# Retention in a two-layer token mixer: 272 keys in tiles of 128, 128 and 16 instead of 128, 72 and 72

## The chip, the cores and the metric

The kernel runs on one core of a Trainium2 chip. The metric is the device time of one execution in microseconds (us), lower is better. TensorE does the matrix products, and what the profile calls PEld is its loading of weights, which overlaps the products. VectorE (DVE), ScalarE (ACT) and GpSimd (POOL) do the elementwise work, and SyncE (SP) issues most transfers. Each engine runs its own list of instructions strictly in order, and waits on semaphores of the others.

## The reference

Two layers run over 272 tokens (16 learned ones, then 256 real ones) of width 2048. Of each layer the change touches the retention, with 8 heads of 128 key columns and 256 value columns:

```python
q = rotary(q, pos) * (RET_DK ** -0.5)
k = rotary(k, pos)
scores = jnp.einsum('bhid,bhjd->bhij', qi, ki) * decay      # causal, decays with i - j
inner  = jnp.einsum('bhij,bhjv->bhiv', scores, vi)
y_ret  = head_group_norm(retention, gn_g) * silu(g_ret)
...
merged = sigmoid(m_ret) * (y_ret @ w_branch[0]) + sigmoid(m_conv) * (y_conv @ w_branch[1])
h      = h + merged @ w_out
```

The reference goes through chunks with a carried state; the kernel computes the same thing over all pairs (i, j) with j <= i at once. All projections (q, k, v, the gates and the convolution's inputs) come from one 2048 x 18432 matrix per layer. Everything is float32.

## The kernel before, in words

The tokens stand along the free dimension. The work is a list of **blocks**, one for each 128 output columns of a weight matrix. A block loads its 128 x 2048 weights in two halves (`raw`), splits each into a rounded high part `wh` (a ScalarE copy, L127) and a rest `wl` (a VectorE subtraction, L128), and runs 48 or 32 matmuls over 16 slices of the input (L153, L156, L170). TensorE works through the blocks one after the other. The weights of a block are loaded and split two blocks ahead.

For each head of a layer there are six blocks (k, q, two of v, two of gates). After the first gate's block come the `scores`, after the second the `outputs` (in head 0 of layer 0 both are put two blocks later, `LATE`). Within `scores`:

- L291 makes the scores of the first 128 keys with three products of split operands (`products3`, L250). The other keys go through plain float32 products (L295): weights are the keys of a tile (72 columns), and the moving operand is the queries from the tile's first key on (144, then 72 columns). Each appears in the trace as two matmuls, each with its own weight load.
- L299 and L300 multiply by the decay and write `sc`. L300 does tiles 2 and 3 with one instruction: 72 partitions, 144 + 72 = 216 columns.
- L307 transposes the values with TensorE, two transposes for each tile; the weights are the tile's tokens (128 or 72 columns), and 128 columns of an identity move.
- L311 (ScalarE) and L312 (VectorE) take the mean out of each tile's values, and `halves` splits the first tile's (`hi<-v` on ScalarE, `lo<-v` on VectorE).

In `outputs`, for each half of the value columns, three split products of the first tile (L250: weights `hi`, `hi`, then `lo` of the values) and two plain float32 products for tiles 2 and 3 (L327: weights are 72 x 128 values, 144 and 72 columns of `sc` move) add up in one PSUM bank.

The table `JT` holds, for each tile, the first key, the number of keys and the column where its scores begin in `sc`; `SC` is the number of columns of `sc` and of the decay table `dec`, 128 x `SC` for each head.

The order in which an engine runs its instructions is not that of the source: the framework lays it out when it builds the program, by its own estimate of when each instruction can start. A change of a shape can so move other instructions.

Of the kernel before, what the change touches and what calls it, by code (L numbers as in the profile page):

```python
# [18 lines left out]
L = SEQ + META  # L19
# [6 lines left out]
EPS = 1e-6  # L26
HALF = KC // 2

JT = ((0, 128, 0), (128, 72, 272), (200, 72, 416))
SC = 488  # L30


FIRST = 4
# [16 lines left out]
def hybrid_trunk(ctx: ExitStack, tc: tile.TileContext, xT, w_first, w_in, w_br, w_out, w_last, g_last, params, consts, dec, out):  # L50
# [13 lines left out]
    def new(name, cols=L):  # L64
        return tmp.tile([P, cols], F32, tag="t", name=name, padded_shape=[P, L])
# [78 lines left out]
    def product(parts, mov, c0, spare=False, narrow=False, midway=None):  # L144
        n = L - c0
        ps = psr.tile([P, 512], F32, name="pr") if spare else psm.tile([P, 512], F32, name="ps")
        if 2 * n <= 512 and not narrow:

            both = ps.rearrange("p (m n e) -> p m n e", m=2, e=2)
            for k in range(KC):  # L150
                wh, wl = parts[k // HALF]
                o = (k % HALF) * P
                nc.tensor.matmul(  # L153
                    both, wh[:, o:o + P], mov[:, k, :, :, c0 // 2:].rearrange("p e m n -> p m n e"), start=(k == 0), stop=False, skip_group_check=True
                )
                nc.tensor.matmul(  # L156
                    turns(ps[:, :n]), wl[:, o:o + P], part(mov, k, 0, c0),
                    start=False, stop=(k == KC - 1), skip_group_check=True,
                )
            b, a = new("pb", n), new("pa", n)  # L160
            nc.scalar.copy(b, ps[:, n:])  # L161
            nc.vector.tensor_tensor(out=a, in0=ps[:, :n], in1=b, op=ALU.add)  # L162
            return a
        for k in range(KC):
            if k == HALF and midway:
                midway()
            wh, wl = parts[k // HALF]
            o = (k % HALF) * P
            for i, (w, m) in enumerate(((wh, 0), (wh, 1), (wl, 0))):
                nc.tensor.matmul(  # L170
                    turns(ps[:, :n]), w[:, o:o + P], part(mov, k, m, c0),
                    start=(k == 0 and i == 0), stop=(k == KC - 1 and i == 2),
                )
        return ps[:, :n]
# [7 lines left out]
    def tt(out, a, b, op=ALU.mult):  # L182
        nc.vector.tensor_tensor(out=out, in0=a, in1=b, op=op)  # L183
# [53 lines left out]
    def halves(a, cols, moving=False):  # L237

        hi, lo = newr("hi", cols), newr("lo", cols)
        if moving:  # L240
            a, hi, lo = apart(a), hi.rearrange("p (e n) -> p e n", e=2), lo.rearrange("p (e n) -> p e n", e=2)
        nc.scalar.copy(hi, a)
        tt(lo, a, f32(hi), ALU.subtract)
        if moving:
            hi, lo = hi.rearrange("p e n -> p n e"), lo.rearrange("p e n -> p n e")
        return hi, lo

    def products3(out, w, m, stop=True):
        for i, (a, b) in enumerate(((0, 0), (0, 1), (1, 0))):
            nc.tensor.matmul(turns(out), w[a], m[b], start=(i == 0), stop=(stop and i == 2))  # L250

    def retention(layer, hd, i0, u, y):
# [33 lines left out]
        def scores():  # L286
            dt = decp.tile([P, SC], F32, name="dec")
            nc.sync.dma_start(dt, dec[hd])
            ps = psr.tile([P, 512], F32, name="pr")
            sc = scp.tile([P, SC], F32, name="sc")  # L290
            products3(ps[:, i0:L], st["kr"], st["qr"])  # L291
            for j0, nj, o in JT[1:]:
                lo = max(j0, i0)
                o += lo - j0
                nc.tensor.matmul(  # L295
                    ps[:nj, o:o + L - lo], st["k"][:, j0:j0 + nj], st["q"][:, lo - i0:L - i0],
                    start=True, stop=True,
                )
            tt(sc[:, i0:L], ps[:, i0:L], dt[:, i0:L])  # L299
            tt(sc[:72, L:SC], ps[:72, L:SC], dt[:72, L:SC])  # L300
            st["sc"] = sc
            st["scr"] = halves(sc[:, i0:L], L - i0, moving=True)
            pv = [psr.tile([P, 512], F32, name="pr") for _ in range(2)]
            vt = [pv[0][:, :DV], pv[0][:, DV:], pv[1][:, :DV]]
            for n, (j0, nj, _) in enumerate(JT):
                for c in range(2):
                    nc.tensor.transpose(vt[n][:nj, c * P:(c + 1) * P], st["v", c][:, j0:j0 + nj], ident)  # L307
            vv = []
            for n, (j0, nj, _) in enumerate(JT):
                v, sm = new("v", DV), new("vsum", 1)  # L310
                nc.scalar.activation(v[:nj], vt[n][:nj], AF.Copy, accum_out=sm[:nj])  # L311
                nc.vector.tensor_scalar(  # L312
                    out=v[:nj], in0=v[:nj], scalar1=float(DV), scalar2=sm[:nj], op0=ALU.mult, op1=ALU.subtract
                )
                vv.append(v)
            st["vr"] = halves(vv[0], DV)
            st["vc"] = vv

        def outputs():
            for c in range(2):  # L320
# [3 lines left out]
                )  # L324
                for n, (j0, nj, o) in enumerate(JT):
                    if n > 0:
# [32 lines left out]
        block(wl[VB + 2 * hd + 1], u, 0, val(1))  # L359
        block(wl[GB + 2 * hd], u, i0, gate(0))  # L360
        after_last(scores, late)
        block(wl[GB + 2 * hd + 1], u, i0, gate(1))
        after_last(outputs, late)
# [217 lines left out]
    for k0, nk in START:  # L581
# [18 lines left out]
        for w, m in ((wh, 0), (wh, 1), (wl, 0)):  # L600
            for n in range(FIRST):
                for k in ks:
                    o = ((k - k0) * FIRST + n) * P
# [25 lines left out]
    for b, (_, mov, c0, done) in list(enumerate(blocks))[FIRST:]:  # L629
        ps = product(  # L630
            ready.pop(b), mov, c0, spare=(b < FIRST + 2), narrow=(b == len(blocks) - 1),
            midway=first_scales if b == FIRST else None,
        )
# [13 lines left out]
def _constants():  # L647
# [5 lines left out]
    consts = np.concatenate([cos, sin, np.full((P, P), 1.0 / DV), np.eye(P)], axis=1).astype(np.float32)  # L653
    dec = np.zeros((HEADS, P, SC), np.float64)
    for hd in range(HEADS):
        log_g = np.log(1.0 - 2.0 ** (-5.0 - hd))
        for j0, nj, o in JT:
            diff = np.arange(j0, L)[None, :] - np.arange(j0, j0 + nj)[:, None]
# [69 lines left out]
```

## Time and profile before

| | us |
|---|---|
| median of 3 runs (lowest, highest) | 2156.81 (2156.37, 2156.91) |
| the profiled execution's own time | 2156.63 |
| its span, first to last instruction | 2154.8 |
| TensorE busy | 2143.1 (99%) |
| VectorE busy | 1461.6 (68%) |
| ScalarE busy | 1061.8 (49%) |
| GpSimd busy | 64.0 (3%) |

The busy time of an engine is the time in which at least one of its instructions runs; engines overlap, so the rows don't add up. Matmuls are pipelined, one starts while the one before it still drains, so what a matmul costs in a row of matmuls is the distance from its start to the next one's, and not its duration. The 1.8 us between the span and the execution's time lie around the instructions.

### The profile page before, as it was taken

What the parts mean: (1) busy time and instruction counts of PE and PEld (TensorE: products, weight loads), DVE (VectorE), ACT (ScalarE), POOL (GpSimd) and SP (SyncE); (2) the same over time, 40 slices, a digit from 0 to 9 for tenths busy, and PEclk for the clock granted to TensorE, in tenths of its full rate; (3) what the DMA queues carried; (4) which work ended last, traced back from release to release, by engine and by line L of the source; (5) the groups of instructions that cost most, each with busy time, mean ns of one, the idle gap of its engine ahead of it and who ended that gap; (6) DMA issues with size and microseconds to landing.
All of it is one profiled execution on the core that took longest, in us unless ns stands there. A gap on an engine that the chain in (4) does not pass through costs nothing.

```text
span 2154.8 us, 40227 instructions
## 1 busy us (share of the span) xinstructions
PE 2143.1 (99%) x16623; PEld 2080.3 (97%) x16623; DVE 1461.6 (68%) x2047; ACT 1061.8 (49%) x1474; POOL 64.0 (3%) x100
## 2 busy tenths in 40 slices
PE   9999999999999999999999999999999999999998
PEld 9999999999999999999999999999999999999987
DVE  8877775556666666566677778766677777766765
ACT  6555554334444444444556665654444444445544
POOL 0000000000000000000100000001310000000000
PEclk9999999999999999999999999999999999999999
DMA  8555555555555555555555555556666566556673
GB/s 291 180 179 176 188 177 191 192 189 189 192 189 191 191 188 191 189 189 191 189 188 184 187 182 188 172 203 212 208 219 200 199 200 198 200 201 203 200 224 127
DMA packets 122232, 417.26 MB, mean 194 GB/s; under 512 B 14016, under 2 KB 21568, under 8 KB 122048
## 3 DMA queue, kind: packets, MB, share of 16 engines
q1 hardware_dynamic: 117744, 411.27, 58.4%
q0 software_dynamic: 2048, 2.10, 0.4%
q8 instruction: 130, 2.13, 0.4%
q10 hardware_dynamic: 2256, 1.31, 0.2%
q14 instruction: 54, 0.44, 0.1%
HBM read 410.44 MB, written 2.10 MB: 191 GB/s over the span
## 4 chain that ended last, share of the span: by engine, by line
PE 98%; DVE 1%; ACT 0%; DMA 0%; issue 0%; SPq 0%; DVEq 0%
PE ps L170 62%; PE ps L153 19%; PE ps L156 10%; PE ps L524 4%; PE ps L604 1%; PE pr L250 1%; PE pr L327 1%; PE pr L307 0%; PE pr L295 0%; DVE wl L128 0%; DMA front<-in_xT 0%; PE pr L341 0%; DVE rs L222 0%; ACT front L550 0%; DVE k L183 0%
## 5 line engine op out<-in xcount | busy, mean ns | idle before, releaser
L170 PE MATMUL ps<-act,wh 128*128 128x272 f32 (+1 forms) x7776 | 1349.2, 279 | 0.0
L127 ACT CAST wh<-raw 128x1024 fp32r<-128x1024 f32 x760 | 794.9, 1046 | 985.5 <-PE ps L170 438.9
L128 DVE TENSOR_TENSOR wl<-raw,wh 128x1024 fp32r<-128x1024 f32 x760 | 929.1, 1223 | 513.6 <-ACT wh L127 507.3
L170 PEld LDWEIGHTS ps<-act,wh 128*128 128x128 f32 x7776 | 1184.0, 189 | 0.5
L170 PE MATMUL ps<-act,wl 128*128 128x272 f32 (+1 forms) x3888 | 1082.6, 278 | 0.0
L170 PEld LDWEIGHTS ps<-act,wl 128*128 128x128 f32 x3888 | 735.9, 189 | 0.0
L153 PE MATMUL ps<-act,wh 128*128 128x512 f32 x1904 | 626.7, 382 | 0.0
L156 PE MATMUL ps<-act,wl 128*128 128x256 f32 x1904 | 519.0, 273 | 0.0
L153 PEld LDWEIGHTS ps<-act,wh 128*128 128x128 f32 x1904 | 359.9, 189 | 49.1
L156 PEld LDWEIGHTS ps<-act,wl 128*128 128x128 f32 x1904 | 365.5, 192 | 0.0
L524 PE MATMUL ps<-wh,act 128*128 128x512 f32 x256 | 76.1, 379 | 0.0
L524 PEld LDWEIGHTS ps<-wh,act 128*128 128x128 f32 x256 | 48.3, 189 | 6.8
L162 DVE TENSOR_TENSOR pa<-ps,pb 128x256 f32<-128x256 f32 x119 | 49.7, 417 | 0.6 <-ACT pb L161 0.6
L524 PE MATMUL ps<-wl,act 128*128 128x512 f32 x128 | 48.5, 379 | 0.0
L183 DVE TENSOR_TENSOR gs<-ps,rs 128x272 f32<-128x272 f32 x62 | 27.3, 440 | 25.1 <-PE ps L170 25.1
L161 ACT COPY pb<-ps 128x256 f32<-128x256 f32 x119 | 43.5, 366 | 0.0
L485 POOL DMA_DIRECT2D front<-tr x64 | 37.0, 585 | 178.9 <-DVE tr L479 174.8
L210 POOL TENSOR_TENSOR ss<-ss,sq 128x272 f32<-128x272 f32 x14 | 13.5, 964 | 783.4 <-ACT sq L203 783.4
L344 DVE RECIPROCAL rg<-ysd 128x272 f32<-128x272 f32 (+1 forms) x16 | 28.8, 1803 | 8.6 <-ACT ysd L343 8.6
L391 DVE SCALAR_TENSOR_TENSOR cz<-zp,par,cz 128x272 f32<-128x272 f32 (+1 forms) x64 | 31.4, 490 | 1.1
L335 POOL TENSOR_TENSOR ysq<-ysq 128x272 f32<-128x272 f32 (+1 forms) x16 | 12.7, 796 | 577.7 <-ACT ysq L332 506.7
L183 DVE TENSOR_TENSOR gs<-pa,rs 128x256 f32<-128x256 f32 x64 | 27.1, 423 | 1.6
(126 smaller groups left out, 971.9 us busy)
## 6 DMA issues: line engine op xcount, KB each, us to landing
raw<-in_w_in SPq DMA_DIRECT2D x568, 512.0 KB, 4.6
raw<-in_w_br SPq DMA_DIRECT2D x128, 512.0 KB, 4.7
raw<-in_w_out SPq DMA_DIRECT2D x32, 512.0 KB, 4.8
raw<-in_w_last SPq DMA_DIRECT2D x32, 512.0 KB, 4.3
dec<-in_dec SPq DMA_DIRECT2D x16, 244.0 KB, 3.4
raw<-in_w_first SPq DMA_DIRECT2D x7, 512.0 KB, 7.3
front<-tr POOLq DMA_DIRECT2D x64, 32.0 KB, 4.7
front<-in_xT SPq DMA_DIRECT2D x7, 272.0 KB, 7.4
```

The costliest lines, as they stand in the source:

```text
L127: nc.scalar.copy(wh, raw)
L128: nc.vector.tensor_tensor(out=wl, in0=raw, in1=f32(wh), op=ALU.subtract)
L153: nc.tensor.matmul(both, wh[:, o:o + P], mov[:, k, :, :, c0 // 2:].rearrange("p e m n -> p m n e"), start=(k == 0), stop=False, skip_group ...
L156: nc.tensor.matmul(turns(ps[:, :n]), wl[:, o:o + P], part(mov, k, 0, c0), start=False, stop=(k == KC - 1), skip_group_check=True,)
L161: nc.scalar.copy(b, ps[:, n:])
L162: nc.vector.tensor_tensor(out=a, in0=ps[:, :n], in1=b, op=ALU.add)
L170: nc.tensor.matmul(turns(ps[:, :n]), w[:, o:o + P], part(mov, k, m, c0), start=(k == 0 and i == 0), stop=(k == KC - 1 and i == 2),)
L183: nc.vector.tensor_tensor(out=out, in0=a, in1=b, op=op)
L344: nc.vector.reciprocal(rg, sd)
L391: nc.vector.scalar_tensor_tensor(out=a, in0=z[:, t + i0:t + L], scalar=conv_w(layer, k, t), in1=a, op0=ALU.mult, op1=ALU.add)
L485: nc.gpsimd.dma_start(dst[b, :, a], src[a, :, b])
L524: nc.tensor.matmul(turns(ps), u[:, k, e, m, META // 2:], w[:, c * 512:(c + 1) * 512].rearrange("p (e n) -> p n e", e=2), start=(k == 0 and ...
```

## The change

Tile 2 takes keys 128 to 255 and tile 3 keys 256 to 271. The scores of the tiles have 144 and 16 columns. With 128 and 16 partitions the two tiles no longer form one rectangle, so the decay is multiplied in tile by tile. The tables `sc` and `dec` become 56 columns narrower.

```diff
-JT = ((0, 128, 0), (128, 72, 272), (200, 72, 416))
-SC = 488
+JT = ((0, 128, 0), (128, 128, 272), (256, 16, 416))
+SC = 432
...
             tt(sc[:, i0:L], ps[:, i0:L], dt[:, i0:L])
-            tt(sc[:72, L:SC], ps[:72, L:SC], dt[:72, L:SC])
+            for j0, nj, o in JT[1:]:
+                tt(sc[:nj, o:o + L - j0], ps[:nj, o:o + L - j0], dt[:nj, o:o + L - j0])
```

The code has one line more from here on, so L307, L311, L312 and L327 are L308, L312, L313 and L328 after.

On TensorE, in `scores` of head 0 of layer 0 (the same in all 16 heads; `pr` is the PSUM bank, `q,k` and `con,vT` the operands, partitions x moving columns), the difference is:

```order
 L250 MATMUL pr<-lo,hi 128x272
 L250 MATMUL pr<-hi,lo 128x272
-L295 MATMUL pr<-q,k 72x144
-L295 MATMUL pr<-q,k 72x72
-L307 MATMUL pr<-con,vT 128x128 x2
-L307 MATMUL pr<-con,vT 72x128 x4
+L295 MATMUL pr<-q,k 128x144
+L295 MATMUL pr<-q,k 16x16
+L308 MATMUL pr<-con,vT 128x128 x4
+L308 MATMUL pr<-con,vT 16x128 x2
```

No instruction is added or moved there; shapes change.

On VectorE, in head 0 of layer 0, from the scores on (`gt` and `gs` are the gate, `wl` the split of the weights of a coming block, `lo<-sc` and `lo<-v` the low parts for the outputs), the order before is:

```order
L183 TENSOR_TENSOR sc<-pr,dec 128x272
L183 TENSOR_TENSOR sc<-pr,dec 72x216
L280 SCALAR_TENSOR_TENSOR gt<-gs,par,sg 128x272
L128 TENSOR_TENSOR wl<-raw,wh 128x1024
L183 TENSOR_TENSOR lo<-sc,hi 128x272
L312 TENSOR_SCALAR v<-v,vsum 128x256
L312 TENSOR_SCALAR v<-v,vsum 72x256 x2
L183 TENSOR_TENSOR lo<-v,hi 128x256
L183 TENSOR_TENSOR rot_a<-ps,cosr 128x272
```

and after the change, at the same place:

```order
L183 TENSOR_TENSOR sc<-pr,dec 128x272
L183 TENSOR_TENSOR sc<-pr,dec 128x144
L280 SCALAR_TENSOR_TENSOR gt<-gs,par,sg 128x272
L183 TENSOR_TENSOR sc<-pr,dec 16x16
L183 TENSOR_TENSOR lo<-sc,hi 128x272
L128 TENSOR_TENSOR wl<-raw,wh 128x1024
L313 TENSOR_SCALAR v<-v,vsum 128x256 x2
L313 TENSOR_SCALAR v<-v,vsum 16x256
L128 TENSOR_TENSOR wl<-raw,wh 128x1024
L183 TENSOR_TENSOR lo<-v,hi 128x256
L183 TENSOR_TENSOR rot_a<-ps,cosr 128x272
```

One `wl` stands behind `lo<-sc` instead of ahead of it, and a second `wl`, which came later (after the next head's rotation), now stands ahead of `lo<-v`. In the other seven heads of layer 0 nothing but the split of the `sc` instruction differs. In layer 1's heads the 16 x 16 piece comes behind one addition of the next block, and one `wl` stands behind `lo<-sc` instead of ahead of it; no second one is moved.

On ScalarE, in head 0 of layer 0, the order before is:

```order
L242 CAST hi<-sc 128x272
L311 ACTIVATE v,vsum<-pr 128x256
L311 ACTIVATE v,vsum<-pr 72x256 x2
L242 CAST hi<-v 128x256
L127 CAST wh<-raw 128x1024 x2
```

and after:

```order
L242 CAST hi<-sc 128x272
L312 ACTIVATE v,vsum<-pr 128x256 x2
L312 ACTIVATE v,vsum<-pr 16x256
L127 CAST wh<-raw 128x1024
L242 CAST hi<-v 128x256
L127 CAST wh<-raw 128x1024
```

One of the two `wh` casts now stands ahead of `hi<-v`.

## Rows read from the trace of the kernel before

**Rows 1.** The page: share of the span by engine in the chain that ended last.

```profile
PE 98%; DVE 1%; ACT 0%; DMA 0%; issue 0%; SPq 0%; DVEq 0%
```

**Rows 2.** Waits of TensorE over the whole span: total us, times, longest.

```profile
PE pr L577 <- DVE eps L94: 1.6, 1, 1.6
PE ps L604 <- ACT wh L597: 0.3, 1, 0.3
```

**Rows 3.** Timeline, TensorE, scores of head 1: start, us, count; overlapping stretches.

```profile
73.00 0.54 PE L295 MATMUL pr<-q,k 128*72 128x144 f32 x4
73.25 0.29 PE L295 MATMUL pr<-q,k 128*72 128x72 f32 x2
73.38 0.82 PE L307 MATMUL pr<-con,vT 128*128 128x128 f32 x6
73.38 0.27 PE L307 MATMUL pr<-con,vT 128*128 128x128 f32 x1
```

**Rows 4.** Groups by line and form, weight loads: count, busy us, mean ns, idle before.

```profile
L327 PEld LDWEIGHTS pr<-sc,v 72*128 72x128 f32 x128 | 17.6, 190 | 0.0
L307 PEld LDWEIGHTS pr<-con,vT 128*72 128x72 f32 x64 | 7.0, 115 | 0.1
L307 PEld LDWEIGHTS pr<-con,vT 128*128 128x128 f32 x32 | 3.3, 143 | 0.0
```

**Rows 5.** Timeline, matmuls and weight loads, outputs of head 1, around the 72-column products.

```profile
80.19 0.34 PE L327 MATMUL pr<-sc,v 72*128 72x72 f32 x2
80.33 0.36 PE L250 MATMUL pr<-hi 128*128 128x272 f32 x1
80.19 0.19 PEld L327 LDWEIGHTS pr<-sc,v 72*128 72x128 f32 x1
80.30 0.19 PEld L250 LDWEIGHTS pr<-hi 128*128 128x128 f32 x1
80.41 0.19 PEld L250 LDWEIGHTS pr<-lo,hi 128*128 128x128 f32 x1
```

**Rows 6.** Timeline, VectorE, head 0 of layer 0, from its scores on.

```profile
50.14 0.72 DVE L183 TENSOR_TENSOR sc<-pr,dec 128x272 f32<-128x272 f32 x2
50.78 0.49 DVE L280 SCALAR_TENSOR_TENSOR gt<-gs,par,sg 128x272 f32<-128x272 f32 x1
51.19 1.22 DVE L128 TENSOR_TENSOR wl<-raw,wh 128x1024 fp32r<-128x1024 f32 x1
52.33 0.43 DVE L183 TENSOR_TENSOR lo<-sc,hi 128x272 fp32r<-128x272 f32 x1
52.68 0.87 DVE L312 TENSOR_SCALAR v<-v,vsum 128x256 f32<-128x256 f32 x3
53.49 0.43 DVE L183 TENSOR_TENSOR lo<-v,hi 128x256 fp32r<-128x256 f32 x1
```

**Rows 7.** Timeline, head 0: the first product with `lo` weights, and ScalarE's `hi<-v`.

```profile
54.34 0.28 PE L250 MATMUL pr<-hi,lo 128*128 128x272 f32 x1
53.06 0.41 ACT L242 CAST hi<-v 128x256 fp32r<-128x256 f32 x1 [0.91 <-DVE v L312]
```

**Rows 8.** Timeline, last head of layer 1: `lo<-v`, and the first product of the outputs.

```profile
1383.12 0.43 DVE L183 TENSOR_TENSOR lo<-v,hi 128x256 fp32r<-128x256 f32 x1
1385.57 0.28 PE L250 MATMUL pr<-hi 128*128 128x256 f32 x1
```

**Rows 9.** Timeline, TensorE: two stretches of the opening, and its last matmul.

```profile
4.95 2.15 PE L604 MATMUL ps<-act,wh 128*128 128x272 f32 x8
7.63 1.09 PE L604 MATMUL ps<-act,wh 128*128 128x272 f32 x8
2144.74 0.38 PE L524 MATMUL ps<-wl,act 128*128 128x512 f32 x1
```

**Rows 10.** Busy us by stretch at the end: length, PE, PEld, DVE, ACT, POOL, granted clock, DMA.

```profile
2140.00:2147.00 7.00, 5.12 (x24) 4.16 (x22) 4.54 (x12) 3.54 (x11) 0.00 (x0) 1.00 0.43 124
2147.00:2150.00 3.00, 0.00 (x0) 0.00 (x0) 1.25 (x5) 1.75 (x5) 0.00 (x0) 0.60 0.43 125
```

## The prediction

> **What bounds the kernel now.** I read the chain of work that ended last first: 98% of the span is TensorE's [rows 1]. Then I asked TensorE's waits whether it is ever held up. In the whole span it waits for another engine twice, 1.6 us for its first operands and 0.3 us in the opening [rows 2]; nowhere in the retention. So a nanosecond of matmul spacing saved in a head is a nanosecond off the end, a nanosecond of new waiting is one on it, and work of VectorE and ScalarE is free as long as no operand comes late. The timelines of one head's scores and outputs then give the spacing of the matmuls that change, and those of VectorE against TensorE give how early each operand is ready.
>
> The bar for a difference: 0.2% of 2156.8 is 4.3 us, about what a measurement of this kernel can tell from no change. In 16 heads that is 0.27 us a head, about what all its 72-column products together cost.
>
> **The change, part by part.**
>
> *Scores.* The two 144-column products start at 73.00 and the 72-column ones at 73.25, the first transpose at 73.38 [rows 3]. Each tile's product is two matmuls, so a 144-column matmul costs 0.125 us and a 72-column one 0.065, both 0.87 ns a column. The moving columns set the pace here. By this a 16-column matmul would cost 0.014. The weights are 128 keys wide instead of 72 in tile 2; a float32 load of 128 columns takes 0.11 (below), under the 0.125 of the matmul that covers it, so it costs nothing; were it not covered, it could add at most the 0.05 by which a load grows (56 columns at 0.87 ns). Behind the second 16-column matmul comes the transpose's load of 128 columns. A transpose load of 72 columns takes 115 ns and one of 128 takes 143 [rows 4]: 28 ns for 56 columns, 0.5 ns each, so 0.064 for 128. The second small matmul can therefore not save anything worth a number: its place is held by that load. The pair goes from 0.13 to 0.014 + 0.064 = 0.078, a gain of 0.05 us a head.
>
> The bounds of this gain: nothing, if a matmul however small holds its place for the 0.065 of the smallest seen here; 0.10, if both shrink to 0.014. I take 0.05, since the two sizes in the trace lie on one line through nothing.
>
> [...]
>
> *Transposes.* Six start in 0.82 us less the last one's own 0.27, that is 0.11 apart [rows 3], although two of them have 128 tokens as weights and four have 72. The 128 moving columns of the identity set it (128 x 0.87 = 0.11), and they stay. Four with 128 and two with 16 cost the same: nothing gained or lost.
>
> *Outputs.* Here the weights are 128 columns of values whatever the tile's keys. Around the 72-column products the loads start at 80.19, 80.30 and 80.41, 0.11 apart [rows 5], although 72 columns would need 0.065. The next product's row is drawn out to 0.36 where such a product lasts 0.28 elsewhere [rows 5, 7], which I read as a matmul that started on paper and waited for its weights. So the loads, not the columns, set the pace at the end of `outputs`, and fewer moving columns give nothing. Fewer rows of weights don't either: L327's loads with 72 rows take the same 0.19 as L250's with 128 rows [rows 4, 5]. I take a gain of nothing. Its upper bound: if the loads did not hold them, four 72-column matmuls a head would each fall by 0.05, 0.20 a head.
>
> *The decay multiplication, VectorE.* Two instructions with 488 columns take 50.14 to 50.78, 0.64 us [rows 6]. Three with 432 take between 0.57 (columns alone) and 0.85 (one more instruction at the price of the 216-column one by its share, 0.28). A head has room for this: in the last head of layer 1 `lo<-v` ends at 1383.55 and TensorE asks for the outputs at 1385.57, 2.02 us later [rows 8]. Cost there nothing; if the room were gone, at most 0.2 us a head.
>
> *Head 0 of layer 0, where instructions move.* Here there is no such room. `lo<-v` ends at 53.49 + 0.43 = 53.92, and the product that needs it starts at 54.34 [rows 6, 7]. After the change two weight splits stand ahead of `lo<-v` instead of one. A split holds VectorE from 51.19 to 52.33, 1.14 us [rows 6]. So `lo<-v` ends at 53.92 + 1.14 = 55.06, give or take what the `sc` pieces do (-0.07 to +0.2). ScalarE's `hi<-v` now stands behind a weight cast, but it waited 0.91 us for VectorE anyhow [rows 7]; that is nearly the place the cast fills, so it is not the later one. The product's weights have then to be loaded, 0.11 [rows 5]: it starts at 55.17 instead of 54.34, **a new wait of 0.83 us on TensorE**, bounds 0 (if ScalarE's cast is not ready and VectorE's order costs less than the rows say) to 1.03. Behind it on TensorE is everything else, so it is on the path to the end, once. VectorE is not late for anything behind that: the second split is only taken earlier, and what followed `lo<-v` finds it done. In layer 1 the move puts no more work ahead of `lo<-v`, and 2.02 us are there.
>
> *Transfers.* `dec` shrinks by 56 columns of 4 bytes in 128 rows, 28 KB a head. TensorE waits for no transfer in the retention [rows 2], so nothing.
>
> **The sum.** The gain in head 0's scores is swallowed by its wait, which ends at VectorE's time. Fifteen heads gain 15 x 0.05 = 0.78 us with 0.052 each; head 0 loses 0.83. Net +0.05. On the profiled execution's own time, 2156.63, that is 2156.7; the median of the runs shown is 0.18 higher, so **2156.9**.
>
> [...]
>
> **The rivals.**
>
> [...]
> 2. *The outputs gain too*: loads keep up, and the six 72-column matmuls of a head each fall by 0.05, 0.30 a head, 4.6 us in 15 heads. For it: the product behind the two 72-column ones is recorded at 80.33, 0.14 after the first of them [rows 5], as columns alone would have it. Against it: loads 0.11 apart and the drawn-out row. With the wait, -3.8 us: 2153.0; without the wait too, -4.9: 2151.9, which alone would be faster by over 0.2%.
> 3. *The wait in head 0 does not come*, because the engines' real times leave the second split room elsewhere. Then only the gain is left, 16 x 0.05 = 0.8: 2156.0. Against it: an engine runs its list in order, and the list says so.
> 4. *The other side, slower*: the 0.83 us in which TensorE stands still brings its clock down, at 55 us. At the lower level a group of eight matmuls takes 2.15 us instead of 1.09 [rows 9]. If it stays there as long as in the opening, from 1.6 [rows 2] to 7.63 at most [rows 9], 6 us cost 3 more: 2159.9. It is slower by over 0.2% only from some 8.5 us at that level. Against it: at the end TensorE's last matmul ends at 2145.12 [rows 9], and the granted clock is still full until 2147 and only then falls (0.60 as a mean of the following 3 us) [rows 10]; so two microseconds without any work did not bring it down there.
>
> **How the numbers follow.** The forecast has 0.66, rival 1 0.12, rival 2 0.10, rival 3 0.07, rival 4 0.05. The forecast, 1 and 3 lie between 2155.8 and 2157.8 with the bounds of the wait and the gain, and hold 0.85; the range of 2155.2 to 2158.4 adds the execution's own spread of half a microsecond on each side. Rival 2 with the wait is within 0.2%, and so is rival 4 as priced. Faster by over 0.2% is rival 2 in its full size: 0.03. Slower is rival 4 with a longer stretch: 0.03, and 0.01 for waits that I have not seen. Within 0.2%: 0.93.
>
> **What would show it.** In the profile after: in each head's scores the first transpose starts 0.05 us earlier behind the second 144-column product than before; the transposes stay 0.11 apart; the loads around the 16-column products of the outputs stay 0.11 apart. In head 0 TensorE has a wait of some 0.8 us in front of the product with `lo` weights, released by VectorE's `lo<-v`, and no other wait in the retention. The granted clock stays full there. The forecast is wrong if the retention shows a second wait, if the spacing in the outputs shrinks with the columns, or if the end is off by microseconds although TensorE's rows in the heads are as described.

## The result, and the profile after

The changed kernel takes **2169.32 us** (median of 4 runs, 2168.91 to 2169.32); the kernel before, beside it, takes 2156.61. The ratio is 1.0058, with a 95% interval of 1.0046 to 1.0070: **slower by 12.7 us**, where 2156.9 was forecast. In its page (first three parts) and its waits of TensorE nothing stands out but the longer span:

```profile
span 2167.1 us, 40242 instructions
PE 2155.1 (99%) x16623; PEld 2083.5 (96%) x16623; DVE 1461.4 (67%) x2063; ACT 1062.7 (49%) x1474; POOL 63.2 (3%) x100
...
PEclk9999999999999999999999999999999999999999
```

```profile
PE pr L578 <- DVE eps L94: 1.6, 1, 1.6
PE pr L250 <- DVE lo L183: 0.4, 1, 0.4
PE ps L605 <- ACT wh L598: 0.3, 1, 0.3
```

TensorE runs as many matmuls as before, is busy 12.0 us longer, waits once more for 0.4 us [rows 2], and its clock is at 90% or more of full in every slice (0.999 as a mean of the whole execution). So the time is between matmuls that wait for no other engine. The timeline of TensorE in head 1 says where. Of the kernel before, four rows that were not shown: the block behind the scores, the plain products of the outputs' two halves, and the block behind the outputs:

```profile
73.95 0.36 PE L170 MATMUL ps<-act,wh 128*128 128x272 f32 x1
...
79.94 0.58 PE L327 MATMUL pr<-sc,v 72*128 72x144 f32 x4
...
80.76 0.58 PE L327 MATMUL pr<-sc,v 72*128 72x144 f32 x4
81.15 0.36 PE L170 MATMUL ps<-act,wh 128*128 128x272 f32 x1
```

The same places after:

```profile
74.13 0.55 PE L295 MATMUL pr<-q,k 128*128 128x144 f32 x4
74.62 0.88 PE L308 MATMUL pr<-con,vT 128*128 128x128 f32 x6
75.25 0.36 PE L170 MATMUL ps<-act,wh 128*128 128x272 f32 x1
...
81.24 0.73 PE L328 MATMUL pr<-sc,v 128*128 128x144 f32 x4
...
82.35 0.73 PE L328 MATMUL pr<-sc,v 128*128 128x144 f32 x4
83.01 0.38 PE L170 MATMUL ps<-act,wh 128*128 128x272 f32 x1
```

From the first plain product of the scores to the next block it was 73.95 - 73.00 = 0.95 us [rows 3] and is 1.12, **0.17 more**. From the plain products of one half of the outputs to those of the other it was 0.82 and is 1.11, **0.29 more**; from those of the second half to the next block it was 0.39 and is 0.66, **0.27 more**. The other 15 heads show the same within 0.01 us. Sixteen heads at 0.17 + 0.56 make 11.7 us; with 0.7 for head 0's wait (below) it is 12.4, where the two profiled executions lie 12.3 apart (2156.63 and 2168.91) and the medians 12.7. The expectations below carry 0.585 for the outputs and 0.75 for the head, from taking 0.29 twice.

Inside, the weight loads show how. This is PEld in the first half's outputs, first one load of the kernel before, then the kernel after (start, duration; the 16-row loads one by one):

```profile
80.07 0.19 PEld L327 LDWEIGHTS pr<-sc,v 72*128 72x128 f32 x1
```

```profile
81.58 0.18 PEld L328 LDWEIGHTS pr<-sc,v 16*128 16x128 f32 x1
81.69 0.18 PEld L328 LDWEIGHTS pr<-sc,v 16*128 16x128 f32 x1
81.90 0.19 PEld L250 LDWEIGHTS pr<-hi 128*128 128x128 f32 x1
82.00 0.19 PEld L250 LDWEIGHTS pr<-lo,hi 128*128 128x128 f32 x1
```

The steps tell it: 0.11 from small load to small load, 0.21 from the last small one to the full one behind it, 0.10 among full ones again. Before, from 80.07 on, the three steps were 0.12, 0.11 and 0.11 [rows 5]. The way out of the small products costs 0.10. The way in costs 0.20: before, the second of the tile's two loads started at 80.19, 0.25 us after the first 144-column product at 79.94; now it starts at 81.69, 0.45 after the one at 81.24. That TensorE had to finish first, both times, is a guess of mine; the rows show the later starts and no cause.

### The profile page after: what moved, and what is told of

It reads as the page before. It is cut to its first block, busy times and chain, and to the rows that moved or that the text cites. A ratio compares the mean times of both kernels' runs of the same rounds, so it can differ in the third digit from the quotient of the medians.

```text
span 2167.1 us, 40242 instructions
## 1 busy us (share of the span) xinstructions
PE 2155.1 (99%) x16623; PEld 2083.5 (96%) x16623; DVE 1461.4 (67%) x2063; ACT 1062.7 (49%) x1474; POOL 63.2 (3%) x100
## 4 chain that ended last, share of the span: by engine, by line
PE 97%; DVE 1%; ACT 1%; issue 0%; DMA 0%; SPq 0%; DVEq 0%
PE ps L170 62%; PE ps L153 19%; PE ps L156 10%; PE ps L525 4%; PE pr L250 1%; PE pr L328 1%; PE pr L308 1%; DVE wl L128 0%; PE pr L295 0%; DMA front<-in_xT 0%; ACT wh L598 0%; ACT act L194 0%; PE pr L342 0%; DVE squares L183 0%; PE pr L578 0%
```

## The experiments

Two theories stood against each other, both suppositions of mine. A: TensorE loses time in the change between products whose weights fill few rows or columns and full ones, on the way in and on the way out. That it goes over to another setting of its array there, or empties itself, no row of a trace shows; the runs test where the cost stands. B: 16 moving columns are simply too few to cover anything.

**One key moved from tile to tile (two runs).** The changed kernel with other numbers in its table; 65 keys last, then 64:

```diff
-JT = ((0, 128, 0), (128, 128, 272), (256, 16, 416))
-SC = 432
+JT = ((0, 128, 0), (128, 79, 272), (207, 65, 416))     # then (128, 80, 272), (208, 64, 416)
+SC = 481                                               # then 480
```

> Tiles of 128, 79 and 65 keys: the changed kernel with other numbers in its table, the decay applied tile by tile. Theory A (TensorE empties itself when a product's weights fill so few rows or columns that it goes over to another setting of its array, and again when it goes back): 65 rows and columns still count as the full array, as 72 did, so the time is that of the kernel before, 2156 to 2158 us, and the small products start 0.06 us apart in the scores. Theory B (a moving operand of 16 columns is too short to cover a weight load, wherever it stands): 65 columns are like 72, so also 2156 to 2158. Only with the next run does this tell them apart.

> Tiles of 128, 80 and 64 keys, one key moved against the run before, 64 moving columns instead of 65. Theory A, if half the array is where the setting changes: some 0.6 to 0.75 us a head more than with 65 keys, 2166 to 2169 us, and the first weight load of the small product in scores and outputs starts over 0.3 us after the one before it. If the setting changes only further down, as with 65. Theory B: 64 columns cover what 65 cover, so 2156 to 2158 us.

Measured: 65 keys last 2156.59 us, ratio 1.0 (0.999 to 1.0009); 64 keys last 2171.93 us, ratio 1.0072 (1.0057 to 1.0087). Neither shows head 0's wait. TensorE's plain products in head 1, with 65 and then with 64:

```profile
74.23 0.52 PE L295 MATMUL pr<-q,k 128*79 128x144 f32 x4
74.59 0.82 PE L308 MATMUL pr<-con,vT 128*128 128x128 f32 x6
...
81.16 0.58 PE L328 MATMUL pr<-sc,v 79*128 79x144 f32 x4
...
81.98 0.29 PE L328 MATMUL pr<-sc,v 79*128 79x144 f32 x1
```

```profile
75.72 0.67 PE L295 MATMUL pr<-q,k 128*80 128x144 f32 x4
76.31 0.88 PE L308 MATMUL pr<-con,vT 128*128 128x128 f32 x6
...
82.94 0.77 PE L328 MATMUL pr<-sc,v 80*128 80x144 f32 x4
...
84.09 0.29 PE L328 MATMUL pr<-sc,v 80*128 80x144 f32 x1
```

With 65 the first transpose comes 0.36 us after the first product, with 64 it is 0.59; the halves of the outputs are 0.82 and 1.15 apart. One key is worth 15 us. No moving operand is short here, so B cannot explain it. A's own size was missed: 2171.9 lies above the 2169 that was expected, at 0.95 us a head against the changed kernel's 0.73, which I read as longer small products: 296 ns as a mean in the outputs and 246 in the scores, where those of 16 keys last 268 and 183.

**The same short moving operand, with wider weights (two runs).** The third tile's weights are widened to 65 (then 64) keys, of which all but the last 16 belong to tile 2 and have a decay of zero here; `Q0` keeps the queries from 256 on.

```diff
-JT = ((0, 128, 0), (128, 128, 272), (256, 16, 416))
+JT = ((0, 128, 0), (128, 128, 272), (207, 65, 416))     # then (208, 64, 416)
+Q0 = (0, 128, 256)
...
-                            st["sc"][:nj, o:o + L - j0], start=False, stop=(n == 2),
+                            st["sc"][:nj, o:o + L - Q0[n]], start=False, stop=(n == 2),
...
+            own = np.arange(j0, j0 + nj)[:, None] >= q0
```

> The changed kernel's third tile with 65 keys (207 to 271) as weights, of which 49 are the second tile's and have a decay of zero here, and still only the last 16 queries as moving columns. The result is the same. Theory A: rows and columns count as the full array, so the cost of 0.75 us a head goes away, and with 0.7 for head 0's wait the time is 2156 to 2158 us. Theory B: the moving operand has 16 columns as in the changed kernel, so 2166 to 2170 us.

> The same with 64 keys (208 to 271) in the third tile, one row and one weight column less. Theory A with the setting changing at half the array: back to 2166 to 2170 us, about that of the changed kernel. Theory A with a change only at 32 or less: as with 65. Theory B: 2166 to 2170 us in this run and in the one with 65 alike.

Measured: 65 wide 2157.20 us, ratio 1.0002 (0.9993 to 1.0012); 64 wide 2170.60 us, ratio 1.0065 (1.0050 to 1.0080), 0.6 us above its expectation's end. The timelines of the two in head 1, 65 first:

```profile
73.54 0.48 PE L294 MATMUL pr<-q,k 128*128 128x144 f32 x4
73.87 0.85 PE L307 MATMUL pr<-con,vT 128*128 128x128 f32 x6
74.48 0.36 PE L171 MATMUL ps<-act,wh 128*128 128x272 f32 x1
...
80.47 0.54 PE L327 MATMUL pr<-sc,v 128*128 128x144 f32 x4
...
81.29 0.29 PE L327 MATMUL pr<-sc,v 128*128 128x144 f32 x1
```

```profile
74.63 0.63 PE L294 MATMUL pr<-q,k 128*128 128x144 f32 x4
...
75.82 0.36 PE L171 MATMUL ps<-act,wh 128*128 128x272 f32 x1
...
81.81 0.73 PE L327 MATMUL pr<-sc,v 128*128 128x144 f32 x4
...
82.92 0.41 PE L327 MATMUL pr<-sc,v 128*128 128x144 f32 x2
```

The same 16 columns move in both; 0.82 against 1.11 between the halves. B falls, and A holds with a border between 64 and 65. In the scores the next block starts 0.94 us after the first product with 65 weight columns and 1.19 with 64, where the changed kernel with 16 has 1.12: that 0.07 in 16 heads, 1.1 us, is most of the 1.3 by which the 64-wide kernel is slower than the changed one, which the expectation did not have. The 65-wide kernel is the changed tiling without its loss; it is no faster than the kernel before either.

**Small products one behind the other.** In `outputs` the two 16-key products of a head stand together at the end (`plain(n, c)` is L328's product for tile n and half c):

```diff
             for c in range(2):
...
-                for n, (j0, nj, o) in enumerate(JT):
-                    if n > 0:
...
+                plain(1, c)
+            for c in range(2):
+                plain(2, c)
```

> The changed kernel with the outputs' two 16-key products of a head put one behind the other, after everything else of both halves, instead of one at the end of each half. Nothing else differs. Theory A, cost at the change of setting: one way in and one way out a head are gone. From the trace of the changed kernel a way in delays the weight load by some 0.21 us and a way out by 0.10, so half of the outputs' 0.585 us a head, 4.7 us in all, comes back: 2163.5 to 2165.5 us. Theory C (each small product pays for itself, because its loads can never be prepared): no change, 2168 to 2170 us.

Measured: 2164.87 us, ratio 1.0038 (1.0025 to 1.0051), 4.4 us less than the changed kernel's 2169.3. In head 1:

```profile
81.10 0.41 PE L325 MATMUL pr<-sc,v 128*128 128x144 f32 x2
...
81.69 0.95 PE L325 MATMUL pr<-sc,v 128*128 128x144 f32 x6
82.57 0.50 PE L170 MATMUL ps<-act,wh 128*128 128x272 f32 x2
```

```profile
82.14 0.41 PEld L325 LDWEIGHTS pr<-sc,v 16*128 16x128 f32 x3
```

From the first plain product to the next block it is 1.47 us, where the changed kernel needs 83.01 - 81.24 = 1.77; the 0.30 saved is one way in and one way out (0.20 + 0.10). Three of the four small loads in a row take 0.41 us with the last one's own 0.19, so they start 0.11 apart. The small products are as many and as small as before, so the cost belongs to the change between them and full ones (A), and theory C, a price on each, falls.

**Rows alone, columns alone (two runs).** The kernel with the widened third tile once more; this tile now holds 80 keys, `(192, 80, 416)`. First the scores use all 80 as weight columns and the outputs only the last 16 rows; then the reverse, with the other 64 rows of `sc` set to zero (lines joined and shortened; in the reverse the decay, too, is multiplied into the last 16 rows only).

```diff
-    ps[:, Q0[n] - i0:L - i0], st["vc"][n][:nj, c * P:(c + 1) * P], st["sc"][:nj, o:o + L - Q0[n]], ...
+    ps[:, Q0[n] - i0:L - i0], st["vc"][n][Q0[n] - j0:nj, c * P:(c + 1) * P], st["sc"][Q0[n] - j0:nj, o:o + L - Q0[n]], ...
```

```diff
-    ps[:nj, o:o + L - lo], st["k"][:, j0:j0 + nj], st["q"][:, lo - i0:L - i0],
+    ps[lo - j0:nj, o:o + L - lo], st["k"][:, lo:j0 + nj], st["q"][:, lo - i0:L - i0],
...
+            nc.gpsimd.memset(sc[:64, 416:SC], 0.0)
```

> The third tile holds 80 keys (192 to 271, the first 64 with a decay of zero) in the scores and in the transposes; the outputs take its last 16 rows only (partitions 64 to 79). So the scores' weights have 80 columns and the outputs' weights 16 rows. Theory A with rows and columns each for themselves: the outputs keep their 0.585 us a head (9.4 us), the scores lose their 0.17: 2156.8 + 9.4 + 0.7 for head 0's wait = 2166 to 2168 us. If only columns count: 2156 to 2158. If the starting partition matters too, the outputs' cost differs from 0.585 us a head.

> The reverse: the scores' weights are 16 columns, written to partitions 64 to 79, the outputs take 80 rows of which the first 64 are set to zero by GpSimd. Theory A: the scores keep their 0.17 us a head (2.7 us), the outputs lose theirs: 2156.8 + 2.7 + 0.7 = 2159 to 2161 us. If only rows count: 2156 to 2158 us. This and the run before should add up to the change's whole loss.

Measured: 16 rows 2167.30 us, ratio 1.0048 (1.0032 to 1.0065); 16 columns 2160.96 us, ratio 1.0019 (1.0010 to 1.0029). Timelines of head 1, rows first:

```profile
75.06 0.50 PE L294 MATMUL pr<-q,k 128*128 128x144 f32 x4
75.40 0.85 PE L307 MATMUL pr<-con,vT 128*128 128x128 f32 x6
...
82.00 0.73 PE L327 MATMUL pr<-sc,v 128*128 128x144 f32 x4
...
83.11 0.29 PE L327 MATMUL pr<-sc,v 128*128 128x144 f32 x1
```

```profile
74.10 0.55 PE L294 MATMUL pr<-q,k 128*128 128x144 f32 x4
74.59 0.44 PE L309 MATMUL pr<-con,vT 128*128 128x128 f32 x2
...
81.21 0.54 PE L329 MATMUL pr<-sc,v 128*128 128x144 f32 x4
...
82.03 0.43 PE L329 MATMUL pr<-sc,v 128*128 128x144 f32 x3
```

With 16 rows the outputs keep their 1.11 and the scores are back at 0.34 to the first transpose; with 16 columns the scores keep the changed kernel's 0.49 and the outputs are back at 0.82. Few rows and few columns each do it, and it does not matter that the 16 rows stand at partition 64. The two losses, 10.5 and 4.1 us, add up to 14.6. Each contains head 0's wait (0.6 and 0.7 in their waits); less one of them they make some 13.9 against the change's 12.7, which the intervals (2 us and more to each side) don't tell apart. The spacings in head 1 are those of the changed kernel, each alone.

## Why the prediction was wrong

**The step that failed** is the one on small weights. The forecast asked what sets the pace of the small products (columns that move, or the load of weights) and held the load of 16 rows to be the load of 72 rows: fewer moving columns give nothing, "Fewer rows of weights don't either", and no loss stood beside it. In the scores it let the second small product's place be held by the transpose's load, and did not ask what 16 weight columns do. Each 16-row load is indeed no longer than before, 0.18. But in head 1 the first of them starts 0.22 behind the start of the full product ahead of it (81.58 and 81.36), where a 72-row load started with it (both at 80.07), and the full load starts 0.19 behind the start of the last small product (81.90 and 81.71), where it was 0.05 (80.30 and 80.25). In its place the runs showed a price on the change from full to small weights and back, 0.56 us a head in the outputs and 0.17 in the scores, 11.7 of the 12.7 us. The forecast's own sign, loads around the 16-column products that stay 0.11 apart, fails with it: 0.21. The forecast had no term for a product next to one of another size: its bounds went from nothing to gains. Its nearest rows were loads of 72, which is on the same side of the border as 128. But for 0.05 for a wider load, the bounds of `scores` and `outputs` excluded a loss without a row that excluded it; that is also why the range was far too narrow.

The border between 64 and 65 (15.3 us for one key), the cost in both directions (0.20 us on the way in, and 0.21 us for the step on the way out where 0.11 is usual) and the gain from putting small products together (4.4 us) are measured. Theory A's cause is not: that a setting of the array changes, and that TensorE empties itself for it, was my supposition, and no row of the profile names either. The kernel asks for no setting; here a tile of 64 rows or columns was enough.

**Transposes**, forecast at nothing: right for what they cost themselves. The two with 16 weight columns in head 1, after:

```profile
75.11 0.38 PE L308 MATMUL pr<-con,vT 128*16 128x128 f32 x2
```

They run 0.11 apart as ever (0.38 less the last one's own 0.27), and the next block's full weights follow without a step: its product starts at 75.25, 0.03 behind the second, about as before the change (73.95 against 73.38 + 0.55 [rows 3]). 0.88 us for six in place of 0.82 [rows 3] is the first transpose, which starts 0.16 ahead of the second (74.62 and 74.78) instead of 0.11. So a transpose with few columns does not pay what a product with few columns pays. What sets them apart, and whether the split products (L250) would pay, was not tried.

**Outputs held by the loads**, so that fewer moving columns give nothing: right. With 65 rows of weights and 16 instead of 72 moving columns the halves are 0.82 apart, as before. Rival 2, in which they gain, falls with it.

**Scores, a gain of 0.05 a head**: mis-sized even where the weights stay above the border. With 65 weight columns and 16 moving ones, the first transpose comes 0.05 earlier (0.33 for 0.38 [rows 3]), but the next block starts 0.94 after the first product instead of 0.95: the transposes take nearly all of it back. With 16 weight columns the gain never shows: the sum of gain and loss is the 0.17 above. The bound of no gain, 0.065 for each matmul however small (rival 1, with its chance of 0.12), would have left that first transpose at 0.38, and it falls directly: with 65 weight columns the two 16-column matmuls of head 1 start 0.03 us apart.

```profile
73.78 0.24 PE L294 MATMUL pr<-q,k 128*65 128x16 f32 x2
73.81 0.21 PE L294 MATMUL pr<-q,k 128*65 128x16 f32 x1
```

One small sum of the prediction is off, and nothing hangs on it: six 72-column matmuls at 0.065 are 0.39 us a head and not some 0.27.

**Head 0's wait**: right in place and cause, a little smaller than 0.83. VectorE and TensorE in head 0 after:

```profile
53.19 1.21 DVE L128 TENSOR_TENSOR wl<-raw,wh 128x1024 fp32r<-128x1024 f32 x1
54.32 0.40 DVE L183 TENSOR_TENSOR lo<-v,hi 128x256 fp32r<-128x256 f32 x1
...
54.08 0.28 PE L250 MATMUL pr<-lo,hi 128*128 128x272 f32 x1
54.78 0.38 PE L250 MATMUL pr<-hi,lo 128*128 128x272 f32 x1 [0.43 <-DVE lo L183]
55.00 0.73 PE L328 MATMUL pr<-sc,v 128*128 128x144 f32 x4
```

The second split stands in front of `lo<-v`, which ends at 54.72; the product with `lo` weights starts 0.70 us after its predecessor and its successor 0.22 later, each time in place of 0.12. That is 0.68 us, of which the waits' row counts 0.4. Rival 3, no wait, falls. So does rival 4: behind the wait, from 54 to 62 us, the granted clock (the third number from the right) is 1.00.

```profile
54.00:62.00 8.00, 7.57 (x61) 7.03 (x60) 7.51 (x14) 3.88 (x7) 0.76 (x1) 1.00 0.56 192
```

A slice of the page is 54 us long and would hide 6 us at half clock behind its 9, so this row and not the page answers it. Rival 4 took the opening's level from spacings that halve there [rows 9]; no row shows a lowered granted clock behind them.

**Decay, transfers, the other heads**: no further wait of TensorE in the retention, as forecast.

## What to carry to other kernels

When a tile size changes, look at the rows and columns of the weights of every matmul beside its neighbours', and not only at what moves: here a tile of 16 or 64 rows or columns among full ones cost 0.17 to 0.33 us each time TensorE went into it and out, and 65 cost nothing that the times show. A ragged tile can be widened with rows that count for nothing (2157.20 us here with 65), or small products can be put together so that the change is paid once (4.4 us less here). And where no row of the trace shows an operand of the new size, a loss belongs into the bounds as well as a gain.

## What had not been expected of the hardware

The sharpness: one key moved between two tiles, from 65 to 64, made the kernel slower by 15.3 us (2156.59 to 2171.93). And in the outputs the price does not fall with the rows: with 16 moving columns, 16 rows give the same 1.11 us from half to half as 64 rows; only in the scores are 16 weight columns cheaper than 64 (1.12 against 1.19). Sizes between 16 and 64 were not tried, nor two different small sizes side by side.
